# A small store, 64 bytes of each of 128 output rows, placed among the loads of a convolution kernel

**Chip, cores, metric.** One core of a Trainium2 chip. The metric is the device time of one execution in microseconds (us).

## The reference

A 3x3 convolution with padding 1 and a residual added, in float32, cut to what matters:

```python
x:        16 x 64 x 64 x 64      weight: 64 x 64 x 3 x 3      residual: 16 x 64 x 64 x 64
output[b, co] += weight[co, ci, kh, kw] * x_pad[b, ci, kh:kh+h, kw:kw+w]     # over ci, kh, kw
return output + residual
```

x, residual and output have 16.8 MB each, so 33.6 MB are read and 16.8 MB written.

## The kernel before

The 16 images are worked on in 8 pairs. Row `64 * im + c` of a pair is channel c of image im; it holds 64 x 64 pixels, 16 KB. ScalarE casts x to bf16 (`xr` to `xp`), TensorE convolves into PSUM, and VectorE adds the result into `ro`, where the residual has been loaded. `ro` is then stored. SyncE issues all loads and stores but the first residual load. The parts that matter here:

```python
EARLY = (slice(0, 2), slice(2, 4), slice(4, 6), slice(6, 7))                         # pairs of each big store
RES = (slice(0, 1), slice(1, 2), slice(2, 4), slice(4, 6), slice(6, 8))              # pairs of each residual load
res_bc = residual.rearrange("(p b) c h w -> (b c) p (h w)", b=2)
out_bc = out.rearrange("(p b) c h w -> (b c) p (h w)", b=2)

def store(pairs, cols=slice(0, NPIX)):
    return nc.sync.dma_start(out=out_bc[:, pairs, cols], in_=ro[:, pairs, cols])

for p in range(NPAIR):
    if p >= NXR:
        nc.sync.wait_ge(s_half, 2 * (p - NXR) + 3)       # the x buffer is free again
    ...                                                  # load_x(p); for p == 0 with the weight
    if p in (1, 3, 5, 7):
        load_ro((p + 1) // 2, nc.sync)
for pairs in EARLY:
    nc.sync.wait_ge(s_add, 2 * pairs.stop + 1)           # the adds of these pairs are done
    store(pairs).then_inc(s_out, 16)
...                                                      # the last pair goes out in two halves at the end
```

## Time and profile before

| | before |
|---|---|
| time, median of 3 executions (with a fourth, run beside the changed kernel, 123.00) | 122.98 us |
| span of the profiled execution | 121.2 us |
| bytes moved by DMA | 50.48 MB |
| rate of an undisturbed slice | 433 GB/s |
| busiest compute engine | TensorE, 71% of the span |

The "slices" are the span in 40 equal parts of 3.03 us. The DMA row shows in tenths how busy the 16 DMA engines are; the GB/s row shows what they moved. When DMA is at 9 all along, the GB/s row is the one to read: its low places are where time is lost. The lines are quoted in the prediction.

Two more words on reading. A *packet* is one contiguous piece that one of the 16 DMA engines moves, here mostly a row of 16 KB; a DMA *lands* when its completion is signalled. The views book a packet whole in the stretch in which it starts, so DMA shares can pass 1.00, and the rate of a short stretch is rough: undisturbed stretches of 4 us read 418 to 438 GB/s in this kernel. The trace also holds each packet with its own duration, which the views only show in sums. An undisturbed 16 KB packet takes 611 ns. In the dip they take up to 1359 ns, and what they take beyond 611 ns adds up to 0.71 us for each engine: the same 0.7 us that the rates give, without the roughness. Where the text says "by the packet records", it means such sums, of one profiled execution.

### The profile page before, as it was taken

The page shows a single profiled execution, that of the slowest core. Times are in us where ns is not written, and L with a number is a line of the kernel's source. Part 1 is how long each engine was busy: PE and PEld are TensorE (multiplying, and loading weights), DVE is VectorE, ACT ScalarE, POOL GpSimd, SP SyncE. Part 2 cuts the span into 40 slices and gives each one's busy share as a digit, 9 for nine tenths or more (in the row PEclk, how much of TensorE's full clock was granted, in tenths as well). Part 3 has the DMA queues.
Part 4 walks back from the last instruction along what each step waited for, and adds up shares of the span by engine and source line. Part 5 has one row for each costly group of instructions (what it writes and reads, how often), then busy time and mean ns, then how long its engine had stood idle before and what let it go on. Part 6 is the DMA issues. An engine that isn't in the chain of part 4 may idle for free.

```text
span 121.2 us, 735 instructions
## 1 busy us (share of the span) xinstructions
PE 86.5 (71%) x393; PEld 10.6 (9%) x105; DVE 76.0 (63%) x40; ACT 63.1 (52%) x37; POOL 2.4 (2%) x16
## 2 busy tenths in 40 slices
PE   0000609999999999999999999999999998000000
PEld 0000300010101010101010101010101010000000
DVE  0000180088989889898988989889898988930000
ACT  4001999999999755995785958659200000000000
POOL 5200000000000000000000000000000000000000
PEclk9999999999999999999999999999999999955555
DMA  7999999999999999999999999999999999999994
GB/s 232 416 427 438 433 433 433 427 433 433 433 427 433 427 433 433 433 433 433 433 433 433 433 422 427 384 378 433 433 427 427 433 427 433 433 427 433 416 430 181
DMA packets 3648, 50.48 MB, mean 416 GB/s; under 512 B 320, under 2 KB 448, under 8 KB 448
## 3 DMA queue, kind: packets, MB, share of 16 engines
q1 hardware_dynamic: 3504, 48.38, 94.3%
q10 hardware_dynamic: 144, 2.10, 4.1%
HBM read 33.70 MB, written 16.78 MB: 416 GB/s over the span
## 4 chain that ended last, share of the span: by engine, by line
PE 70%; DVEq 2%; DVE 2%; issue 0%
PE ps L87 52%; PE ps L86 18%; DVEq L130 2%; DVE ro L204 2%
## 5 line engine op out<-in xcount | busy, mean ns | idle before, releaser
L204 DVE TENSOR_TENSOR ro<-ps,ro 64x2048 f32<-64x2048 f32 x32 | 73.2, 2289 | 16.3 <-PE ps L87 15.8
L87 PE MATMUL ps<-xp,wl 128*128 128x504 bf16 (+1 forms) x288 | 78.9, 383 | 0.0
L175 ACT CAST xp<-xr 64x2048 bf16<-64x2048 f32 x16 | 30.3, 1896 | 21.1 <-DMA xr<-in_x_dram 11.7
L86 PE MATMUL ps<-xp,wl 128*128 128x504 bf16 (+1 forms) x96 | 36.9, 384 | 3.4 <-PEq L225 3.4
L179 ACT CAST xp<-xr 64x2048 bf16<-64x2048 f32 x16 | 30.4, 1897 | 0.4
L86 PEld LDWEIGHTS ps<-xp,wl 128*128 128x128 bf16 x96 | 9.4, 98 | 77.8 <-issue 77.8
L191 DVE CAST wl<-ps 32x192 bf16<-32x192 f32 x8 | 2.8, 348 | 14.9 <-PE ps L217 14.8
L217 PE MATMUL ps<-ident,wraw 128*32 128x128 f32 x9 | 2.1, 413 | 12.6 <-DMA wraw<-in_weight_dram 12.6
L217 PEld LDWEIGHTS ps<-ident,wraw 128*32 128x32 f32 x9 | 1.2, 137 | 13.1 <-issue 12.6
L175 ACT ACT_TABLE_LOAD x1 | 1.3, 1283 | 1.1 <-SPq L130 1.1
L184 ACT CAST wl<-ps 32x192 bf16<-32x192 f32 x4 | 1.2, 306 | 0.0
L162 POOL MEMSET xp<- 64x64 bf16 x4 | 0.6, 147 | 0.2
L161 POOL MEMSET xp<- 64x64 bf16 x4 | 0.6, 145 | 0.2
L150 POOL TENSOR_SCALAR_AFFINE_SELECT ident<-ident 128x128 f32<-128x128 f32 x1 | 0.3, 295 | 0.2 <-POOL ident L148 0.2
L164 POOL MEMSET wl<- 64x192 bf16 x1 | 0.3, 253 | 0.1
L163 POOL MEMSET wl<- 64x192 bf16 x1 | 0.3, 252 | 0.1
L148 POOL MEMSET ident<- 128x128 f32 x1 | 0.2, 205 | 0.7 <-SPq L130 0.7
L261 POOL MEMSET const-bfloat16-1.0<- 128x1 bf16 x1 | 0.1, 112 | 0.0
L261 POOL MEMSET const-uint8-127<- 128x1 uint8 x1 | 0.1, 112 | 0.0
L261 POOL MEMSET const-float32-1.0<- 128x1 f32 x1 | 0.1, 109 | 0.0
L261 POOL MEMSET const-float32-0.0<- 128x1 f32 x1 | 0.1, 104 | 0.2 <-issue 0.2
## 6 DMA issues: line engine op xcount, KB each, us to landing
xr<-in_x_dram SPq DMA_DIRECT2D x8, 2048.0 KB, 14.8
ro<-in_residual_dram SPq DMA_DIRECT2D x3, 4096.0 KB, 23.1
out_dram<-ro SPq DMA_DIRECT2D x3, 4096.0 KB, 32.2
ro<-in_residual_dram ACTq DMA_DIRECT2D x1, 2048.0 KB, 12.1
ro<-in_residual_dram SPq DMA_DIRECT2D x1, 2048.0 KB, 20.2
out_dram<-ro SPq DMA_DIRECT2D x1, 2048.0 KB, 15.7
out_dram<-ro SPq DMA_DIRECT2D x2, 1024.0 KB, 11.4
wraw<-in_weight_dram SPq DMA_DIRECT2D x1, 144.0 KB, 11.4
```

Source lines behind the costliest of these rows:

```text
L86: return e.matmul(out=out_, lhsT=lhsT, rhs=rhs, start=start, stop=stop, skip_group_check=True)
L87: return e.add_instruction(mybir.InstMatmult(name=nc.get_next_instruction_name(), engine=PE, ins=[e.lower_ap(rhs), e.lower_ap(lhsT)], outs ...
L130: with tc.tile_critical(no_gpsimd_drain=True):
L161: nc.gpsimd.memset(t[0:64, 0, :], 0.0).then_inc(s_id, 1)
L162: nc.gpsimd.memset(t[64:128, J, :], 0.0).then_inc(s_id, 1)
L175: i = nc.scalar.copy(out=t[64:128, 0:J, :], in_=x4[hp, :, 0, :])
L179: nc.scalar.copy(out=t[0:64, 1 : J + 1, :], in_=x4[hp, :, 1, :]).then_inc(s_pack, 1)
L184: i = nc.scalar.copy(**weight_block(h, *b))
L191: i = nc.vector.tensor_copy(**weight_block(h, *b))
L204: i = nc.vector.tensor_tensor(out=o4[hp, :, par, :], in0=psj[64 * par : 64 * par + 64, :, :], in1=o4[hp, :, par, :], op=ADD)
L217: i = nc.tensor.transpose(out=tp[0:32, t // 3, 128 * (t % 3) : 128 * (t % 3) + 128], in_=wraw3[:, :, t], identity=ident[:, :])
L261: nc = _bacc.Bacc("TRN2", target_bir_lowering=False, num_devices=1)
```

## The change

Its intent, as I read it: to let every DMA engine write to the output once, early and with few bytes, so that the first big store after the loads finds whatever a first store needs. After the residual load of pairs 4 and 5, SyncE stores the first 64 B of each of the first pair's 128 rows. Since those bytes are stored again later, the first big store has to wait for the small one.

```diff
-    def store(pairs, cols=slice(0, NPIX)):
-        return nc.sync.dma_start(out=out_bc[:, pairs, cols], in_=ro[:, pairs, cols])
+    def store(pairs, cols=slice(0, NPIX), lanes=slice(0, 128)):
+        return nc.sync.dma_start(out=out_bc[lanes, pairs, cols], in_=ro[lanes, pairs, cols])
 ...
             if p in (1, 3, 5, 7):
                 load_ro((p + 1) // 2, nc.sync)
+            if p == 5:
+
+                nc.sync.wait_ge(s_add, 3)
+                store(slice(0, 1), slice(0, 16), slice(0, 128)).then_inc(s_out, 16)
+        nc.sync.wait_ge(s_out, 16)
         for pairs in EARLY:
 ...
-        nc.gpsimd.wait_ge(s_out, 16 * len(EARLY))
+        nc.gpsimd.wait_ge(s_out, 16 * len(EARLY) + 16)
```

## The prediction

> **What bounds the kernel now.** I read first the engine shares with the slices of the span, then the chain of work that ended last, the DMA issues, the stretches around one odd place, and last the waits of the issuing queue. Of the page before:
>
> ```profile
> PE 86.5 (71%) x393; PEld 10.6 (9%) x105; DVE 76.0 (63%) x40; ACT 63.1 (52%) x37; POOL 2.4 (2%) x16
> ...
> PEclk9999999999999999999999999999999999955555
> DMA  7999999999999999999999999999999999999994
> GB/s 232 416 427 438 433 433 433 427 433 433 433 427 433 427 433 433 433 433 433 433 433 433 433 422 427 384 378 433 433 427 427 433 427 433 433 427 433 416 430 181
> DMA packets 3648, 50.48 MB, mean 416 GB/s; under 512 B 320, under 2 KB 448, under 8 KB 448
> ```
>
> No engine is full; the DMA row is, from the second slice to the last but one. 50.48 MB at the 433 GB/s of an undisturbed slice is 116.6 us of a 121.2 us span. The other 4.6 us are the start (slice 1 moves 232, so 1.4 us are lost), the end (181 in the last slice, 1.8 us), and one odd place: slices 26 and 27, at 75.75 to 81.81 us, run at 384 and 378. A slice is 3.03 us, so this dip costs ((433 - 384) + (433 - 378)) / 433 x 3.03 = **0.73 us**.
>
> The chain view names PE for 70% (it walks back by semaphores and does not see the DMA backlog), so I checked it against where compute ends. The chain's last pieces:
>
> ```profile
> 102.61 2.28 DVE ro L204
> 104.90 2.33 DVEq L130
> ```
>
> VectorE is done at 107.2 us, the last store lands near 120. Of the DMA issues:
>
> ```profile
> ro<-in_residual_dram SPq DMA_DIRECT2D x3, 4096.0 KB, 23.1
> out_dram<-ro SPq DMA_DIRECT2D x3, 4096.0 KB, 32.2
> ...
> out_dram<-ro SPq DMA_DIRECT2D x2, 1024.0 KB, 11.4
> ```
>
> A 4 MB transfer needs 9.7 us at 433 GB/s, yet takes 23.1 and 32.2 from issue to landing: it queues behind earlier ones. The last two 1 MB stores need 2.4 us each and take 11.4. So the queue is some 7 us deep even when compute has ended. **The bound is the sum of the DMA queue**: bytes, plus stalls inside it. A change counts only by what it does to that sum; waits of SyncE count only if they let the queue run empty.
>
> What is the dip? In the timeline of the SyncE queue the last residual load (4 MB) is issued at 58.23 us and the first store at 58.71. By the landing times of the residual tile's issues, that load lands 23.1 us later, at 81.3, and the store 32.4 us later, at 91.1. So the dip lies where the queue passes from loads to stores. The stretches show it:
>
> ```profile
> 70.00:77.00 7.00, 7.00 (x34) 0.78 (x8) 5.81 (x4) 4.24 (x4) 0.00 (x0) 1.00 1.02 438
> 77.00:80.50 3.50, 3.50 (x18) 0.39 (x4) 3.47 (x2) 3.48 (x2) 0.00 (x0) 1.00 0.96 323
> 80.50:90.00 9.50, 9.50 (x46) 1.07 (x11) 8.28 (x5) 3.79 (x2) 0.00 (x0) 1.00 1.01 435
> ```
>
> The last column is GB/s, the one before it the DMA share. The share stays at 0.96 while the rate falls to 323: packets take longer, the queue is not empty. After it, stores run at 435, like the loads. It is a one-time stall, and I take it that the change is aimed at it: a tiny first store pays it early.
>
> **What the Trainium skill says.** (1) "DMA: Bandwidth & Descriptors", Specifications: 435 GB/s is the fabric ceiling, and transfers under 512 B are a read-modify-write. The trace agrees with the first (433 to 438); no packet of data that small is in it, since the 320 small ones are 16 completions for each of the 20 DMAs. The stored runs are 64 B, so this may bear on the added cost. (2) The same page, "Queues, rings and completion order": on each DMA engine descriptors are consumed in ring order. The trace agrees as far as landings go in order of issue. So the small store runs behind what SyncE issued before it, not at its issue. (3) The same page, "Two DMAs through the same engine are not ordered": two stores to the same bytes need the completion semaphore between them, which is the added wait. (4) "HBM Reference", Latency: 0.2 us on average, 2 us under high load; I use it only as a sign that a small write in a full queue may take a microsecond. No page explains a first-store stall.
>
> **The change part by part.**
>
> *Removed:* nothing. All bytes are still stored, the 64 B runs twice.
>
> *The added store.* Its listing against the kernel before shows one row more of 128x16 on SyncE, between the residual load of the sixth pair and the x load of the seventh, and one added wait at the first big store; PE, DVE, ACT and POOL run the same instructions. It waits for three first-half adds. The first add starts at 24.81 us and images come every 5.19 us, so the third is done near 24.81 + 2 x 5.19 + 2.29 = 37.5 us. SyncE issues the preceding residual load at 38.07, done at 38.50. So the wait is met, and 0.4 us of issue fits before the next x issue at 48.61. Cost on SyncE: none.
>
> *Its time in the queue.* The residual load before it lands 23.1 us after 38.07, at 61.2. So the small store runs near 61 us. Bytes: 128 x 64 B = 8 KB, 0.02 us. Packets: 128, or 8 for each of 16 engines, and 16 completions. What small packets cost, the weight load tells: 128 packets of 1152 B land within 9 to 12.5 us, where the slices show 427 and 438, so no loss above 0.05 us can be seen. Writes of 64 B may be dearer; I set 0.1 us for them, and call that an estimate.
>
> *The added wait.* The first big store, issued at 58.71 before, is now held until the small one lands, near 62 us by the above, one more microsecond if it stalls. At that time the queue still holds the two x loads and the last residual load, which run to 80.5. Slack 18 us. Cost: none.
>
> *The dip.* If the stall is a cost of each DMA engine's first write to the output, it goes from 77-80 us to about 58-62 us. The queue is as full there as here. PE is not near a limit at either place, and a stall there delays all that queues behind it, so moving saves nothing by itself. It saves only if a stall of tiny writes is cheaper than one of 16 KB rows, or if reads flow while a small write waits. Half of it kept is my middle guess: -0.73 + 0.37 + 0.1 = **-0.26 us**. If it is kept whole: +0.1 us.
>
> **Rivals.**
>
> *Moved, not removed.* The cold stall appears near 60 us at its full 0.7 us. For it: the DMA row is at 9 in every slice, so there is no idle time to hide it in. Time 123.0 to 123.2. Chance 40%.
>
> *Mostly saved.* First-use costs are paid by packets of 64 B while the loads' reads are outstanding. For it: the start's first loads are slow as well and the later ones not, which looks like a first-use cost, and stores after the dip run at 435 although each goes to new addresses 4 MB on. Time 122.3 to 122.6. Chance 35%.
>
> *Paid twice.* The dip is not a first write but the switch of the queue from loads to stores, or something in the last load itself. For it: 77 to 80.5 us lies mostly before the store's own data, as the load lands only at 81.3. Then it stays, and the small store adds switches of its own to and fro, up to another 0.7 us. Time 123.2 to 123.8. Chance 25%.
>
> *The queue runs empty* because SyncE waits for the small store. Against it: the 18 us of slack. This would be over 124 us; I give it 1%.
>
> **Range and chances.** Weighted: 0.4 x 123.1 + 0.35 x 122.45 + 0.25 x 123.5 = 122.97; the middle is nearer to 122.9, and I take **122.9 us**. The spread of the stories is 122.3 to 123.8 and runs scatter by 0.1, so 8 in 10 lie in 122.3 to 123.6. Two per cent are 2.46 us, over three times the whole dip: faster by that 1%, slower by that 2%, within 97%.
>
> **What would show it.** Right: the engines' busy times and the 5.19 us beat are unchanged, packets rise by 144 to 3792, the small store lands near 61 to 62.5 us, VectorE still ends near 107.2. The GB/s row then tells the stories apart: "moved" has slices 26-27 at 427-433 and a dip of equal area in slices 20-21; "mostly saved" has the first without the second; "paid twice" has both. Wrong: a slice with the DMA digit well under 9 between slices 3 and 39 (the queue ran empty), a later end of VectorE, or a dip far larger than 0.7 us at the small store, which would mean that small writes stall the queue in a way that nothing in this trace shows.

## The result, and the profile after

The changed kernel takes 123.02 us (123.01 to 123.09, 4 executions), the kernel before 123.00 (122.86 to 123.02, 4 executions). The ratio is 1.0006, with a 95% interval of 0.9988 to 1.0023: no difference.

The page of the changed kernel, DMA rows of the slices and the packet count:

```profile
DMA  7999999999999999999999999999999999999994
GB/s 238 427 427 427 432 432 432 432 432 432 432 432 432 432 432 432 421 432 432 429 427 432 432 432 432 367 367 432 427 427 432 427 432 432 432 432 427 427 427 184
DMA packets 3792, 50.49 MB, mean 416 GB/s; under 512 B 464, under 2 KB 592, under 8 KB 592
```

The 144 packets more are there. The small store runs in slices 20 and 21 (429 and 427): no dip, and by the packet records no 16 KB packet that starts between 58 and 64 us takes over 611 ns. Slices 26 and 27 still have theirs, at 367 and 367. The stretches around it, in the same columns as in the prediction (stretch, length, busy time of PE, PEld, DVE, ACT, POOL, granted clock, DMA share, GB/s):

```profile
70.00:77.00 7.00, 6.95 (x33) 0.78 (x8) 5.81 (x4) 4.24 (x4) 0.00 (x0) 1.00 1.02 438
77.00:80.50 3.50, 3.50 (x18) 0.41 (x5) 3.47 (x2) 3.37 (x2) 0.00 (x0) 1.00 0.97 318
80.50:90.00 9.50, 9.50 (x46) 1.06 (x12) 8.28 (x5) 3.79 (x2) 0.00 (x0) 1.00 1.03 440
```

318 GB/s against 323: the dip is in the same place and no smaller (by the packet records 0.81 us against 0.71). Two things did move, and cost nothing. The SyncE queue's timeline after (start, us until the group ends, what was issued):

```profile
38.42 0.47 SPq L80 DMA_DIRECT2D out_dram<-ro  x1
48.47 9.61 SPq L72 DMA_DIRECT2D xr<-in_x_dram  x2
58.12 0.43 SPq L77 DMA_DIRECT2D ro<-in_residual_dram  x1
61.30 47.00 SPq L80 DMA_DIRECT2D out_dram<-ro  x6
```

The small store is issued at 38.42 and the DMA issues put 22.9 us between its issue and its landing, so it lands at 61.3 us, and the first big store follows at 61.30 instead of 58.71. SyncE's waits show the added one:

```profile
SPq L80 <- DMA out_dram<-ro: 2.7, 1, 2.7
```

2.7 us of waiting in the queue's issuer, and none of it counts: the first big store lands 29.9 us after its issue, at 91.2, against 91.1 before.

### The profile page after: what moved, and what is told of

It reads as the page before. It is cut to its first block, busy times and chain, and to the rows that moved or that the text cites. A ratio compares the mean times of both kernels' runs of the same rounds, so it can differ in the third digit from the quotient of the medians.

```text
span 121.3 us, 733 instructions
## 1 busy us (share of the span) xinstructions
PE 86.3 (71%) x389; PEld 10.6 (9%) x105; DVE 76.0 (63%) x40; ACT 63.1 (52%) x37; POOL 2.4 (2%) x16
## 2 busy tenths in 40 slices
DMA packets 3792, 50.49 MB, mean 416 GB/s; under 512 B 464, under 2 KB 592, under 8 KB 592
## 4 chain that ended last, share of the span: by engine, by line
PE 69%; DVEq 2%; DVE 2%; issue 0%
PE ps L87 53%; PE ps L86 17%; DVEq L130 2%; DVE ro L209 2%
## 5 line engine op out<-in xcount | busy, mean ns | idle before, releaser
L87 PE MATMUL ps<-xp,wl 128*128 128x504 bf16 (+1 forms) x288 | 78.9, 383 | 0.2
L86 PE MATMUL ps<-xp,wl 128*128 128x504 bf16 (+1 forms) x92 | 35.4, 385 | 3.4 <-PEq L230 3.4
## 6 DMA issues: line engine op xcount, KB each, us to landing
out_dram<-ro SPq DMA_DIRECT2D x3, 4096.0 KB, 29.9
```

The source lines that it names most:

```text
L86: return e.matmul(out=out_, lhsT=lhsT, rhs=rhs, start=start, stop=stop, skip_group_check=True)
L87: return e.add_instruction(mybir.InstMatmult(name=nc.get_next_instruction_name(), engine=PE, ins=[e.lower_ap(rhs), e.lower_ap(lhsT)], outs ...
```

## The experiments

So the small store is almost free and the dip does not care about it. The question is what the dip is. I had three stories to begin with: it belongs to the passing of the queue from loads to big stores (A); it belongs to the last residual load (B); the first large writes are dear (C).

**1. The first big store held until the last load has landed.**

```diff
+        nc.sync.wait_ge(s_r[0], 48)
         for pairs in EARLY:
```

> The kernel before, but SyncE issues the first big store only when the last residual load has landed (some 81 us). Theory A, the dip belongs to the passing of the queue from loads to big stores (the store's work reaches ahead into the last load's packets): with no store queued behind the load, the rate at 77 to 80.5 us is 425 or more, the load lands near 80.6, and instead there is an empty gap of some 2 us before the first store; time 123.0 - 0.7 + 2 = 124 to 125 us. Theory B, the dip belongs to the last load itself (its addresses, or that moment): 77 to 80.5 us stays near 320 GB/s although no store is queued, and the time is 124.5 to 125.5. Theory C, the first large write of each DMA engine is dear: 77 to 80.5 us clean, and the first packets after 82 us take over a microsecond.

Measured: 123.95 us, ratio 1.0085 (1.0070 to 1.0100). The stretches of the kernel before, then of this one:

```profile
77.00:79.50 2.50, 2.50 (x13) 0.29 (x3) 2.47 (x2) 2.48 (x2) 0.00 (x0) 1.00 1.03 328
79.50:82.00 2.50, 2.50 (x13) 0.29 (x3) 1.92 (x2) 1.13 (x2) 0.00 (x0) 1.00 0.98 413
```

```profile
77.00:79.50 2.50, 2.50 (x13) 0.29 (x3) 1.93 (x2) 1.63 (x1) 0.00 (x0) 1.00 1.01 433
79.50:82.00 2.50, 2.50 (x14) 0.29 (x3) 2.47 (x2) 2.16 (x2) 0.00 (x0) 1.00 0.29 125
```

With no store queued behind it, the same load runs at 433 where it ran at 328. In its place stands an empty gap (DMA share 0.29), and that costs more. So in this kernel the dip lies in the last load's time but is set off by the store queued behind it: B is refuted, and A fits. (This is one profiled execution; the first kernel of experiment 8 shows the same.) C, slow first packets after the gap, is not seen: the first packets of the store take 608 to 656 ns, 0.07 us too much in all.

**2. The last two loads exchanged**, so that the x load of the last pair comes last.

```diff
             else:
+                if p == 7:
+                    load_ro(4, nc.sync)
                 load_x(p)
-            if p in (1, 3, 5, 7):
+            if p in (1, 3, 5):
```

> The kernel before with its last two loads exchanged: the x load of the last pair now comes after the last residual load. Theory A (passing from loads to stores): the dip stays at 77 to 80.5 us, 123.0 us. Theory B (addresses of the last residual load): it moves 4.9 us earlier, to 72 to 76 us, 123.0 us. VectorE still ends within 0.5 us of 107.2, since the x load lands near 81 and is needed near 87.

Measured: 122.96 us, ratio 0.9995 (0.9981 to 1.0010). The dip stays where it was:

```profile
70.00:77.00 7.00, 7.00 (x34) 0.78 (x8) 5.87 (x3) 4.29 (x3) 0.00 (x0) 1.00 1.00 428
77.00:80.50 3.50, 3.50 (x18) 0.39 (x4) 3.42 (x2) 0.00 (x0) 0.00 (x0) 1.00 1.01 346
```

It is a matter of the place in the queue, not of addresses, and B falls for a second time.

**3. The first pair's rows stored whole in the midst**, 2 MB, once and not again.

```diff
-    EARLY = (slice(0, 2), slice(2, 4), ...
+    EARLY = (slice(1, 2), slice(2, 4), ...
...
+            if p == 5:
+                nc.sync.wait_ge(s_add, 3)
+                store(slice(0, 1)).then_inc(s_out, 16)
...
```

> The place of the change, but the whole of the first pair's rows (2 MB, 16 KB each) is stored there, once, and not again. Theory A (each passing from loads to big stores costs 0.73 us): a dip near 57 to 60 us and a second one near 77 to 80 us, 123.7 us in all. Theory C (only the first big writes of the engines are dear): a dip near 57 to 60 us alone, none at 77 to 80, 123.0 us. Theory B (the last load): only the dip at 79 to 85 us, in the last residual load's packets, 123.0 us.

Measured: 123.37 us (123.08 to 123.53), ratio 1.0035 (1.0023 to 1.0047).

```profile
57.00:61.00 4.00, 4.00 (x21) 0.42 (x5) 3.90 (x2) 3.79 (x2) 0.00 (x0) 1.00 0.97 336
77.00:86.00 9.00, 9.00 (x43) 0.98 (x10) 7.78 (x5) 8.88 (x6) 0.00 (x0) 1.00 0.99 424
```

The dip now lies ahead of this store, and the second passing from loads to stores, at 86 us, has none. So it is paid **once in an execution**, and A's "each passing" is wrong. This is the pattern that was written down for C; but by experiment 1 a first big store is not slow by itself. A big store pays it, the 64 B store does not; moving it saves nothing. The time should then have been the same, and it is 0.4 us longer. The profiled execution was one of the two fastest (123.15) and shows 0.1 us of that in its span; where the rest lies I did not find.

**4. Sixteen small stores instead of one.**

```diff
-                store(slice(0, 1), slice(0, 16), slice(0, 128)).then_inc(s_out, 16)
+                for k in range(16):
+                    store(slice(0, 1), slice(16 * k, 16 * k + 16), slice(0, 128)).then_inc(s_out, 16)
...
```

> The change with sixteen small stores of 64 B runs instead of one, at different columns, all before the first big store. The changed kernel's trace has its 64 B packets at 11 ns each, 8 per engine, so one small store takes 0.09 us of each engine plus a completion of 9 ns, and sixteen take 1.6 us. If that is the full cost, the time is 123.0 + 1.5 = 124.5 us, and the dip at 77 to 80 us comes some 1.5 us later. If small packets cost more than they show (a read-modify-write), over 126 us. If they overlap with loads' packets, 123.0 to 123.3.

Measured: 126.49 us, ratio 1.0291 (1.0277 to 1.0305): 3.6 us more, not 1.5. The timeline of the SyncE queue and the stretches say why:

```profile
38.48 23.09 SPq L80 DMA_DIRECT2D out_dram<-ro  x16
61.62 0.90 SPq L72 DMA_DIRECT2D xr<-in_x_dram  x2
```

```profile
60.00:62.40 2.40, 2.40 (x13) 0.29 (x3) 1.82 (x2) 1.04 (x1) 0.00 (x0) 1.00 0.71 82
62.40:64.00 1.60, 1.60 (x10) 0.20 (x2) 1.57 (x2) 1.57 (x2) 0.00 (x0) 1.00 0.90 205
```

Between 60 and 62.4 us the small stores run, but the DMA share of 0.71 says that the engines also stood idle, so the 2.4 x (431 - 82) / 431 = 1.9 us lost there is not the price of sixteen stores. By the packet records the 64 B packets took 11 ns each as in the changed kernel: 8 x 11 + 9 = 97 ns of each engine for one store (9 ns is its completion), at most 1.55 us for sixteen. That is the price I had put on one. The rest comes from a held issuer. SyncE could not issue its sixteen DMAs in a row: the first ones took 0.43 us each, single later ones up to 12.8 us, and the x load that went out at 48.6 before goes out at 61.62, when the queue has run dry. So each engine was without a load's packet for 2.36 us in all, and the first loads after that are slow (205 GB/s, 0.72 us by the packet records), as at the start of the kernel. And the late dip is still there, larger than before:

```profile
80.50:82.00 1.50, 1.50 (x9) 0.19 (x2) 1.03 (x1) 0.24 (x1) 0.00 (x0) 1.00 1.01 328
82.00:90.00 8.00, 8.00 (x39) 0.88 (x9) 7.25 (x4) 3.79 (x2) 0.00 (x0) 1.00 1.00 391
```

By the packet records it is 1.06 us against 0.71. So 2.36 + 0.72 + 0.35 = 3.4 us of the 3.5 us by which the span grew are found. 8 KB for each engine in 64 B packets did not pay the dip, though here the queue ran dry in between. The time is the one that I had written down for small packets that cost more than they show ("over 126 us"), but the reason is another.

**5. How much has to be stored?** The 64 B store gives each engine 512 B. Three kernels give it 4 KB, 16 KB and 16 KB, in different packets; one look each.

```diff
-                store(slice(0, 1), slice(0, 16), slice(0, 128)).then_inc(s_out, 16)
+                store(slice(0, 1), slice(0, 128), slice(0, 128)).then_inc(s_out, 16)     # 512 B of each row
+                store(slice(0, 1), slice(0, 512), slice(0, 128)).then_inc(s_out, 16)     # or 2 KB of each row
+                store(slice(0, 1), slice(0, NPIX), slice(0, 16)).then_inc(s_out, 16)     # or 16 whole rows
```

> The changed kernel with 512 B of each row in the small store instead of 64 B: 4 KB for each of 16 engines. So far: a 64 B store in the midst shows no dip and leaves the late one whole; a store of whole rows shows the dip and the late one is gone. Theory V (volume: the dip is the time in which an engine first reads ahead of its writes some 0.7 us x 26.8 GB/s = 19 KB of stored data, and keeps that lead): a dip near 57 to 60 us of 4 KB / 26.8 GB/s = 0.15 us and a late one of 0.55 us. Theory S (a store needs packets over some size to set it off): either no early dip and a late one of 0.7 to 0.8 us, or a whole early one and no late one. Time 123.0 to 123.3.

> The same with 2 KB of each row: 16 KB for each engine, in 8 packets. Theory V: an early dip near 0.6 us and a late one near 0.1 us. Theory S: all or nothing at either place. The bytes are 256 KB more, 0.6 us: 123.6.

> The same with whole rows of 16 KB, but only the first 16 rows: one packet of 16 KB for each engine, 256 KB as in the run with 2 KB of each row. Theory V: as there, an early dip near 0.6 us, a late one near 0.1. Theory S by packet size: one big packet sets it off whole, 0.7 early and none late; theory S by number of packets: no early dip, a late one of 0.7. Time 123.6 in each.

Measured: 123.29, 123.43 and 123.28 us, one execution each, against 122.93 for the kernel before. To add up all that is lost, wherever it lies, I compare the rate in two long stretches, 20 to 56 us (loads only) and 56 to 90 us. Before, then 512 B, 2 KB, and 16 rows:

```profile
20.00:56.00 36.00, 36.00 (x166) 4.00 (x41) 27.53 (x13) 30.80 (x18) 0.00 (x0) 1.00 1.01 431
56.00:90.00 34.00, 34.00 (x159) 3.80 (x39) 30.31 (x14) 22.70 (x12) 0.00 (x0) 1.00 1.01 422
```

```profile
20.00:56.00 36.00, 36.00 (x159) 3.90 (x39) 26.54 (x12) 30.55 (x17) 0.00 (x0) 1.00 1.00 423
56.00:90.00 34.00, 34.00 (x159) 3.87 (x40) 29.77 (x14) 22.90 (x13) 0.00 (x0) 1.00 1.01 429
```

```profile
56.00:90.00 34.00, 34.00 (x159) 3.81 (x40) 30.09 (x14) 22.77 (x12) 0.00 (x0) 1.00 1.01 427
```

```profile
56.00:90.00 34.00, 34.00 (x159) 3.84 (x40) 29.77 (x14) 22.76 (x12) 0.00 (x0) 1.00 1.01 427
```

Before, 34 x (431 - 422) / 431 = 0.71 us are lost. With 16 KB for each engine, in either form, 0.32 us: under half. But those bytes are stored twice, and 256 KB more are 0.6 us, so nothing is won. Neither theory's numbers hold: V had put most of the loss at the early place, S all of it at one. With 512 B there is a surprise: 0.16 us at 56 to 90, but 36 x (431 - 423) / 431 = 0.67 us among the loads at 20 to 56, part of it before the small store was even issued. By the packet records the slow packets of that execution are spread from 20 to 61 us, up to the small store's own packets; they add up to 0.74 us, as much as the usual dip, and 0.26 of it lies before 38.9 us, while the small store was issued at 39.53.

**6. 512 B again, timed.** The kernel is the same.

> The run with 512 B of each row again, timed. Its one look had early slow packets of 0.12 us in all per engine and no late dip at all, but slow packets of 0.41 us at 26 to 50 us, before the small store was even issued, and 123.29 us. If those are chance, the dip that is gone is worth 0.73 - 0.12 and the 64 KB more cost 0.15: 122.93 - 0.46 = 122.4 to 122.6 us. If the 0.4 us comes back in this place or another in most executions, the dip's time is only moved: 122.9 to 123.3.

Measured: 123.11 us (122.83 to 123.17), ratio 1.0012 (0.9999 to 1.0026). In the profiled execution the loss is back in its usual place:

```profile
20.00:56.00 36.00, 35.90 (x159) 3.98 (x40) 27.13 (x12) 30.74 (x17) 0.00 (x0) 1.00 1.00 431
56.00:90.00 34.00, 33.95 (x159) 3.80 (x39) 29.77 (x14) 22.78 (x12) 0.00 (x0) 1.00 1.01 424
```

That is 0.55 us. The missing dip was one execution's, and a rule built on it ("512 B is the threshold") would have been wrong.

**7. 512 B of 16 rows only**: the bytes of the change, in packets eight times as long.

```diff
+                store(slice(0, 1), slice(0, 128), slice(0, 16)).then_inc(s_out, 16)
```

> 512 B of each of the first 16 rows only: one packet of 512 B for each engine, 8 KB in all, the same bytes as in the change but in packets eight times as long and an eighth as many. Theory S by packet size (the first writes that are not small set off and pay the one-time cost): the late dip is gone or under 0.3 us, and the time is 122.2 to 122.5, below both kernels. Theory V or any by volume (the 64 B store did nothing because 512 B for each engine is too little): the late dip stays at 0.7 to 0.8 us, 122.9 to 123.1.

Measured: 122.94 us, ratio 1.0007 (0.9993 to 1.0021).

```profile
56.00:90.00 34.00, 33.95 (x159) 3.80 (x39) 30.26 (x14) 22.78 (x12) 0.00 (x0) 1.00 1.01 425
```

That is a loss of 0.47 us. The time, and a dip that stays, are the expectation of a volume, not of a packet size: 512 B for each engine is too little in packets of either length. But 0.47 lies between the two expectations (under 0.3, and 0.7 to 0.8). By the packet records it is 0.49, and single executions of the other kernels that keep the dip have 0.62 to 0.81. So the small store may have taken a part of it; that is not shown.

**8. The release of the first big store timed**, in two ways: by a later add (`s_add >= 11` instead of 5), and by cutting the last load in three and waiting for the first two pieces.

```diff
-            nc.sync.wait_ge(s_add, 2 * pairs.stop + 1)
+            nc.sync.wait_ge(s_add, 11 if pairs.start == 0 else 2 * pairs.stop + 1)
```

> The kernel before, with the first big store released by the eleventh image's first add (78.97 us in the trace of before) instead of at 58.71: it then reaches the DMA queues near 80 us, just as the last load's last packets run (80.2 to 80.5 without a dip), not early enough to read ahead of them and not so late that the queue runs empty as it did when the store waited for the load's landing. If the dip is lost only because the store reads ahead too early, the rate at 77 to 80.5 us is 425 or more, no gap follows, and the time is 122.2 to 122.5. If the loss comes with the passing from loads to stores however it is timed (theory V: the lead must be built once), a gap or slow packets of 0.5 to 0.9 us stand at 80 to 82 us instead, and the time is 122.8 to 123.2.

```diff
+                if p == 7:
+                    nc.sync.wait_ge(s_r[0], 32)
+                    for pair, cols, s in ((6, slice(0, NPIX), s_part), (7, slice(0, 3072), s_part), (7, slice(3072, NPIX), s_r[0])):
+                        nc.sync.dma_start(out=ro[:, pair, cols], in_=res_bc[:, pair, cols]).then_inc(s, 16)
...                                                                                     # else: the load as before
+        nc.sync.wait_ge(s_part, 32)
         for pairs in EARLY:
...
+                if p == 6:
+                    nc.vector.wait_ge(s_part, 32)
```

> The kernel before with the last residual load cut in three (pair 7 but one, the first 12 KB of the last pair's rows, the last 4 KB of them), the first big store released when the first two have landed, so that its packets reach the queues about when the last piece's do end (1.2 us of data left, against some 1.3 us from landing to first packet, as the held store took 0.95 us from issue to first packet). The release by an add came too late (80.17 us, since compute ran about a microsecond later in that execution) and left an empty gap. If the dip is only lost by a store that stands behind the load too early: rate at 77 to 80 us over 420, no gap over 0.2 us, 122.2 to 122.5. If passing over costs it however timed: 122.8 to 123.3, with the loss seen in slow packets or a gap near 80 us.

Measured: the first 123.48 us, scattered from 122.86 to 123.94, ratio 1.0046 (1.0020 to 1.0072). Its release came at 80.17 us, since compute began about 1.2 us later in that execution, and the queue ran empty as in experiment 1. The load itself had no dip, again:

```profile
77.00:79.50 2.50, 2.50 (x13) 0.29 (x3) 1.92 (x2) 1.64 (x1) 0.00 (x0) 1.00 1.02 439
79.50:82.00 2.50, 2.50 (x14) 0.29 (x3) 2.47 (x2) 2.15 (x2) 0.00 (x0) 1.00 0.54 223
```

The second took 122.91 us, ratio 1.0001 (0.9988 to 1.0015). Its timeline of the SyncE queue and its stretches:

```profile
79.55 30.43 SPq L81 DMA_DIRECT2D out_dram<-ro  x6
```

```profile
76.00:77.50 1.50, 1.50 (x8) 0.19 (x2) 0.92 (x1) 0.13 (x1) 0.00 (x0) 1.00 1.01 418
77.50:79.00 1.50, 1.50 (x8) 0.20 (x2) 1.50 (x1) 1.50 (x1) 0.00 (x0) 1.00 0.89 341
80.00:80.50 0.50, 0.50 (x4) 0.00 (x0) 0.50 (x1) 0.50 (x1) 0.00 (x0) 1.00 0.72 295
```

The store is issued at 79.55, yet packets are slow from 77 to 79 us, ahead of the load's last piece with its 4 KB runs. By the packet records this is 0.17 us for each engine (12 KB packets take up to 699 ns where 460 is usual): a quarter of the usual dip, **without any store in the queue**. Then, near 80.3 us, the engines stood without data for 0.3 us, so this release was still a little late and the passing without a gap was not tested. Together with the look of experiment 5 this suggests, on one execution each, that a store queued behind is one thing that sets the loss off, not the only one.

**9. 2 KB of each row in the midst, once.** The bytes of experiment 5's second kernel, but not stored again: the rest of those rows follows after the loads.

```diff
-    EARLY = (slice(0, 2), slice(2, 4), ...
+    EARLY = (slice(1, 2), slice(2, 4), ...
...
+            if p == 5:
+                nc.sync.wait_ge(s_add, 3)
+                store(slice(0, 1), slice(0, 512)).then_inc(s_out, 16)
+        store(slice(0, 1), slice(512, NPIX)).then_inc(s_out, 16)
         for pairs in EARLY:
...
```

> The first 2 KB of each row of the first pair are stored in the midst, as in the run with 2 KB, but not again: the rest of those rows goes out in the first store after the loads. No bytes are added. In the look with 2 KB the packets lost 0.2 us per engine between 56 and 90 us beyond their bytes, against 0.5 in the kernel before. If that holds in most executions, the time is 122.9 - 0.3 = 122.6 us and it beats both kernels by a quarter of a per cent. If the one-time loss comes back, at 77 to 80 us or anywhere, as it did in the second run with 512 B, 122.8 to 123.1.

Measured: 122.71 us (122.62 to 122.73), against 122.86 (122.76 to 122.97) for the kernel before in the same rounds; ratio 0.9984 (0.9970 to 0.9997).

```profile
56.00:90.00 34.00, 33.95 (x158) 3.90 (x40) 29.96 (x14) 22.77 (x12) 0.00 (x0) 1.00 1.01 426
```

34 x (431 - 426) / 431 = 0.39 us lost, against 0.71. (The expectation's 0.2 and 0.5 us for the 2 KB look and the kernel before were counted by another measure; by this one they are 0.32 and 0.71.) The gain in time is 0.15 us, half of what I expected, but all five executions are below all nine of the kernel before. It is the only version whose interval lies below the kernel before, by a sixth of a per cent and barely: one such interval among the nine timed changes is weak evidence. It was not run beside the changed kernel.

## Why the prediction was right or wrong

The time was right: 122.9 predicted, 123.02 measured, within 122.3 to 123.6, and "within 2%". The way there was half right, so a good part of that is luck.

- *The bound is the sum of the DMA queue.* Held. Everything that changed the time did so through that queue: an empty stretch (experiments 1, 4, 8), bytes stored twice (5), or a smaller dip (9). Only the 0.4 us of experiment 3 are not traced to it. The added wait of 2.7 us did not count. Packets rose to 3792 and VectorE ended at 107.1 us, as the signs of being right had it.
- *The small store runs near 61 us, costs SyncE nothing, and 0.1 us in the queue.* Held: it lands at 61.3, and by the packet records takes 97 ns of each engine. The extra microsecond that the prediction allowed for, on the strength of a latency under load, did not appear.
- *The dip.* This step failed. The prediction took the stall as "a cost of each DMA engine's first write to the output" and set -0.73 + 0.37 for moving and halving it. Each engine did write first, near 60.5 us, and the dip stayed whole: that term of the sum was 0, and the time changed by a ratio of 1.0006 where the sum of parts had -0.26 us. What the runs showed in its place is a loss of some 0.7 us, once in an execution, that a big enough store sets off. By the packet records it is 0.71 us before; 0.81 and 0.49 stay late when 512 B for each engine are stored early, and 0.62 with 4 KB; with 16 KB 0.3 to 0.4 are lost in all, early and late; 128 KB move it whole.
- *The rivals.* "Moved, not removed" got the greatest chance and did not happen, nor did "mostly saved". Of "paid twice" the first half happened (the dip stays) and the second did not (the small store adds no dip). The true outcome, dip stays and small store nearly free, was not among the rivals by itself. The time came out right because every story about a 0.7 us dip stays near 123 us: it could not tell a right story from a wrong one. That is the luck.
- *Its sums.* The start, the end and the dip make 1.4 + 1.8 + 0.73 = 3.9 us, not the 4.6 that they were said to explain; the other 0.7 us lie in slices a little under 433. And the sum of parts, -0.26, leads to 122.7 us and the weighted rivals to 122.97; the 122.9 that was stated is neither.
- *The clue was on the table.* The prediction noted that the dip lies mostly before the store's own data, and gave the story that follows from it only 25%.

What stays open: the mechanism. That the engines read ahead of their writes and must build that lead once (theory V) fits the "once" and the dependence on volume. It does not fit the sizes of experiment 5, nor the two losses without a store (part of the first 512 B look, and the split load). No view shows the read and write sides of a DMA engine apart. Nearly all of this rests on one profiled execution of each kernel. The 0.4 us of experiment 3 are open too.

## What to carry to other kernels

When the DMA queue is full from end to end, price a change by what it adds to or takes from that queue, and ignore waits of the issuing engine as long as the queue does not run dry. A one-time stall need not be cured by touching early whatever one believes to be cold: find out first what sets it off, by taking the suspect away (here: hold the store back), and check that a saving isn't just the loss moved elsewhere. Do not build a rule on one profiled execution; the second run of the same kernel may put the loss back.

## What the Trainium skill lacked or had wrong

- "DMA: Bandwidth & Descriptors", Specifications, says that transfers under 512 B are a read-modify-write. That is not tested here. What the page lacks is the price of small stores: a store of 128 runs of 64 B took 97 ns of each DMA engine (11 ns a packet), and the late dip stayed with stored runs of 64 B and of 512 B.
- The same page says nothing of a one-time loss when big stores first queue up behind loads: some 0.7 us in this kernel, at 323 instead of 435 GB/s, in the packets ahead of the store.
- The same page, "Queues, rings and completion order", has no limit on how far the issuing engine can run ahead. With sixteen small stores behind a full queue SyncE was held for most of 23.09 us, single issues took up to 12.8 us instead of 0.43, and the queue ran dry.
- No page that I read gives the whole gap that a queue has when SyncE issues a store only after a load has landed. Here the DMA engines were without data for 1.5 us each (experiment 1), and the kernel took 1.0 us more.
